# Stacked high and low halves for 512-column matmuls in the feed-forwards, and another order of the first expert tiles

## The chip, the cores and the metric

One core of a Trainium2 chip runs the whole program. The metric is the device time of one execution in microseconds (us), as a median of several runs; the profile is one further execution. TensorE (PE in the profile) multiplies, VectorE (DVE), ScalarE (ACT) and GpSimd (POOL) work elementwise, SyncE (SP) issues nearly all DMAs.

## The reference

A token sequence (256 tokens of width 1024) passes through five blocks. What is computed, cut to its core:

```python
x = x + hybrid_mixer(rms_norm(x))            # state-space part and attention, gated, three output projections
h = rms_norm(x)
gi = argmax(h @ w_rg); top2 of the 8 experts of that group
x = x + sum_over_experts(comb * (silu(h @ w_gate[e]) * (h @ w_up[e])) @ w_down[e])   # 32 experts, 2 a token
x = rms_norm(x + sigmoid(rms_norm(x) @ w_ple_gate) * (p @ w_ple))
for i, kind in enumerate((0, 1, 2, 0)):      # short conv, neighborhood attention, hyena, short conv
    x = x + mixer[kind](rmsnorm(x))
    x = x + (silu(g) * u) @ w2               # g, u = split(rmsnorm(x) @ w13); 1024 -> 2 x 2816 -> 1024
```

All of it is float32.

## The kernel before

Activations lie with features on the partitions and the 256 tokens along the free axis; a tile `(128, 2, 256)` holds a pair of feature blocks `o`. Weights are one stream `wst` in DRAM in the order of use. A tile of the stream is 128 x 1024 floats (512 KB): eight 128 x 128 blocks.

**Precision.** A float32 product is made of three matmuls in the fp32r format. A value is split into a high part (ScalarE, a copy that rounds) and a low part (VectorE, value minus high part): weights into `wh`, `wl`, activations into `hh`, `hl`. Each block then costs `wh*hh + wh*hl + wl*hh`, three matmuls of 256 columns with a weight load each (`dense`, line 690). `dense` goes over output pairs `j`; each has one PSUM bank out of four (`mm`), and for every input block `k` and `o` in 0, 1 it takes the next weight block (`block`, line 597). `evac` takes the bank away at the pair's end. While the norm of the input (`norm`, whose factor is applied to the output) isn't there, finished pairs are held.

**The feed-forward** (`ffn`, line 1856) is a dense of 22 pairs over 8 input blocks (`w13`: 22 x 16 = 352 weight blocks) and one of 4 pairs over 22 (`w2`: 176). After each `w13` pair VectorE multiplies the bank by the norm factor (`t`), ScalarE takes Silu of one half, VectorE multiplies the halves, and the result is split (`fh`, `fl`). After `w2`, `residual` (line 876) adds to `x` and prepares the next input and its sum of squares.

**Order.** The program is emitted by Python against a rough clock of its own. Side work (generators in `sides`) is emitted between matmuls by `pump`. Each engine then runs its own list in that order, and semaphores join them.

**Weight buffers.** `raw` has 7 buffers, `wh` and `wl` 5 each, `slots` 46 general ones of 128 x 512. `load_parts` (line 507) issues the next tile of the stream to SP.

**Experts.** In `moe` (line 1433) weights are used unsplit, as moving operand of plain float32 matmuls with 32 stationary columns, four side by side. The experts run in 8 rounds of 4; a round takes 8 tiles (`gate_up(r, 0)`), the 8 down tiles of the round before, and 8 more (`gate_up(r, 1)`). There are 192 tiles. While the router runs, tiles are loaded ahead: `early` (line 534) takes the first 13 free places of the stream in pairs of slots (`raws`), the raw buffers the next 7, and once the last dense is over the 5 + 5 split buffers hold raw tiles too. A tile used up from `raw`, `wh` or `wl` is loaded anew at once (`used_up`); one from slots is not.

Routing is a chain: last residual, `route_pair` (line 1413: transposes, then logits), norm factor, some 25 small VectorE steps to `sel`, counts (`cnt`), places (`ph`), gathers (`hg`), first `gate_up`. Work of the hyena filters (`filters`, line 2111) is stepped in by `next(filt)`, as 24 `fl` matmuls for two orders. `weights(0)` (matmul `cs`) stands in the middle of round 0. `past` (line 1577) reads the largest expert load and branches over a fallback on every engine; it stands at the start of round `r == 2`, after `moe_back` of the round before.

Of the kernel before, what the change touches and what calls it, by code (L numbers as in the profile page):

```python
# [271 lines left out]
NEARLY, EGAP = 13, 1.5  # L272
# [141 lines left out]
class Net:  # L414
    def __init__(self, ctx, tc, a, taps=None):
# [33 lines left out]
        self.nload = self.nsplit = self.ahead = 0  # L449
# [57 lines left out]
    def load_parts(self, parts, kind="raw"):  # L507
        if self.nload < len(self.order):
# [14 lines left out]
    def load_slots(self):  # L523

        c, half = self.order[self.nload]
        t = [self.new("raws", shape=(128, 512)) for _ in range(2)]
        self.raw[self.nload], self.kind[self.nload] = t, "slots"
        self.nload += 1
        self.ahead += 1
        for i in range(2):  # L530
            o = half * 1024 + i * 512
            self.nc.sync.dma_start(t[i], self.a["wst"][c][:, o:o + 512])

    def early(self, n):

        while self.nload < self.moe_tiles[0]:
            yield
        for _ in range(n):
            self.load_slots()
            t0 = self.now()  # L540
            while self.now() < t0 + EGAP:
                yield
# [147 lines left out]
    def dense(self, xh, xl, nk, npairs, evac, j0=0, norm=None, lead=1):  # L690
# [4 lines left out]
        for js in [range(j0, j0 + lead)] + [(j,) for j in range(j0 + lead, j0 + npairs)]:  # L695
            pss = [self.mm_tile("mm") for _ in js]
            for k0 in range(0, nk, 2):
                for ps in pss:
                    for k in (k0, k0 + 1):
                        a, b = xh(k), xl(k)  # L700
                        self.fill(a, b)
                        for o in range(2):
                            wh, wl = self.block()
                            for i, (w, x) in enumerate(((wh, a), (wh, b), (wl, a))):
                                nc.tensor.matmul(ps[:, o, :], w, x, start=(k == 0 and o == 0 and i == 0),
                                                 stop=(k == nk - 1 and i == 2), skip_group_check=True)
# [4 lines left out]
            held += zip(js, pss)  # L711
# [7 lines left out]
    def dense_halves(self, xh, xl, ready, evac):  # L719

        nc = self.nc
        pss = [None] * 4
        for hf in range(2):
            self.wait(lambda: ready(hf))
            for j in range(4):
                if hf == 0:
                    pss[j] = self.mm_tile("mm")
                for k in range(4 * hf, 4 * hf + 4):
                    a, b = xh(k), xl(k)
                    self.fill(a, b)  # L730
                    for o in range(2):
                        wh, wl = self.block()
                        for i, (w, x) in enumerate(((wh, a), (wh, b), (wl, a))):
                            nc.tensor.matmul(pss[j][:, o, :], w, x, start=(k == 0 and o == 0 and i == 0),
                                             stop=(k == 7 and i == 2), skip_group_check=True)
# [3 lines left out]
    def dense_rows(self, xh, xl, evac, chs):  # L739
        nc = self.nc  # L740
        for ch in chs:
            pss = [self.mm_tile("mmr", (128, 512)) for _ in range(2)]
            for k in range(8):
                wh, wl = self.block(512)
                for t in range(2):
                    a, b = xh(k)[:, t * 128:t * 128 + 128], xl(k)[:, t * 128:t * 128 + 128]
                    for i, (x, w) in enumerate(((a, wh), (a, wl), (b, wh))):
                        nc.tensor.matmul(pss[t], x, w, start=(k == 0 and i == 0), stop=(k == 7 and i == 2))
# [3 lines left out]
    def half(self, tiles):  # L752
        def f(k):
            if tiles[k // 2] is None:
                self.wait(lambda: tiles[k // 2] is not None)
            return tiles[k // 2][:, k % 2, :]
# [3 lines left out]
    def split_pair(self, src, scales, hi, lo):  # L760
        nc = self.nc
        for o in range(2):
            nc.scalar.activation(hi[:, o, :], src[:, o, :], AF.Copy, scale=scales[o])
        for o in range(2):
            nc.vector.scalar_tensor_tensor(lo[:, o, :], src[:, o, :], scales[o], hi[:, o, :].bitcast(F32),
                                           op0=ALU.mult, op1=ALU.subtract)
# [5 lines left out]
    def split_pair_steps(self, src, scales, hi, lo):  # L772
        nc = self.nc
        for o in range(2):
            nc.scalar.activation(hi[:, o, :], src[:, o, :], AF.Copy, scale=scales[o])
        yield
        for o in range(2):
            nc.vector.scalar_tensor_tensor(lo[:, o, :], src[:, o, :], scales[o], hi[:, o, :].bitcast(F32),
                                           op0=ALU.mult, op1=ALU.subtract)
# [29 lines left out]
    def prep_input(self, j, scales):  # L809
        if j == 0:  # L810
            self.hh, self.hl = [None] * 4, [None] * 4
        h, l = self.new("hh", F32R), self.new("hl", F32R)
        self.split_pair(self.x[j], scales, h, l)
        self.hh[j], self.hl[j] = h, l
# [8 lines left out]
    def gains(self, name, i, j):  # L823
        return [self.v(name, 8 * i + 2 * j + o) for o in range(2)]

# [56 lines left out]
    def setup(self):  # L882
# [11 lines left out]
        ps = self.sd("warm", (128, 128))  # L894
        for _ in range(WARM):
            nc.tensor.matmul(ps, self.ones, self.ones, start=True, stop=True)
# [81 lines left out]
    def hybrid(self):  # L978
        nc, v = self.nc, self.v
        V, S, G = nc.vector, nc.scalar, nc.gpsimd  # L980
        hh, hl = self.half(self.hh), self.half(self.hl)
# [37 lines left out]
        oh, ol = [None] * 4, [None] * 4  # L1019
# [17 lines left out]
        self.dense(hh, hl, 8, 1, lambda j, ps: tables.append(self.side(first(ps))))  # L1037
        self.side(self.ssd(hh, hl, X, BC, y))
        early = []
        self.dense_rows(hh, hl, lambda *a: early.append(a), (0,))  # L1040
# [6 lines left out]
        self.dense(hh, hl, 8, 2, evac, 1, norm=norm)  # L1047
# [1422 lines left out]
```

## Time and profile before

| | us |
| --- | --- |
| median of 3 runs (1856.04 to 1856.8) | 1856.15 |
| profiled execution | 1855.08 |
| its span, first to last instruction | 1853.3 |
| PE busy | 1784.5 (96%) |
| DVE busy | 1155.6 (62%) |
| ACT busy | 952.7 (51%) |
| POOL busy | 413.3 (22%) |

The page gives busy time by engine, 40 slices of the span with clock and DMA rate, and the chain of work that ended last. Busy spans of matmuls overlap, since they are pipelined: what a matmul costs in a stream is read from the distance of starts, not from its duration. PEclk is the granted TensorE clock, 1.00 for 2.4 GHz and 0.50 for 1.2 GHz.

### The profile page before, as it was taken

What the parts mean: (1) busy time and instruction counts of PE and PEld (TensorE: products, weight loads), DVE (VectorE), ACT (ScalarE), POOL (GpSimd) and SP (SyncE); (2) the same over time, 40 slices, a digit from 0 to 9 for tenths busy, and PEclk for the clock granted to TensorE, in tenths of its full rate; (3) what the DMA queues carried; (4) which work ended last, traced back from release to release, by engine and by line L of the source; (5) the groups of instructions that cost most, each with busy time, mean ns of one, the idle gap of its engine ahead of it and who ended that gap; (6) DMA issues with size and microseconds to landing.
All of it is one profiled execution on the core that took longest, in us unless ns stands there. A gap on an engine that the chain in (4) does not pass through costs nothing.

```text
span 1853.3 us, 34155 instructions
## 1 busy us (share of the span) xinstructions
PE 1784.5 (96%) x13779; PEld 1606.7 (87%) x13779; DVE 1155.6 (62%) x1603; ACT 952.7 (51%) x1515; POOL 413.3 (22%) x452
## 2 busy tenths in 40 slices
PE   9999999998888899999999999999899999999999
PEld 8897899542326899999987999998899999999999
DVE  6677665322125987665697666569976655676653
ACT  7887653331225655444566644466554444655442
POOL 4636340342441340000122000027610000500000
PEclk9999999899899999999999999999999999999999
DMA  8443359699998575555554455555345555555552
GB/s 295 148 132 120 128 182 337 251 362 406 409 406 296 166 243 183 183 183 185 180 165 135 131 184 183 176 193 196 129 129 189 183 183 181 183 180 185 182 185 77
DMA packets 115210, 377.39 MB, mean 204 GB/s; under 512 B 12480, under 2 KB 22088, under 8 KB 115048
## 3 DMA queue, kind: packets, MB, share of 16 engines
q1 hardware_dynamic: 114856, 375.03, 59.2%
q8 instruction: 109, 1.79, 0.4%
q14 instruction: 53, 0.43, 0.1%
q0 software_dynamic: 48, 0.13, 0.0%
q10 hardware_dynamic: 144, 0.00, 0.0%
HBM read 369.87 MB, written 5.25 MB: 202 GB/s over the span
## 4 chain that ended last, share of the span: by engine, by line
PE 66%; DMA 8%; DVE 2%; issue 2%; POOL 1%; ACT 1%; SPq 0%; POOLq 0%; DVEq 0%; ACTq 0%
PE mm L400 59%; DMA raw<-in_wst 8%; PE mmr L400 1%; PE ci L400 1%; PE s L400 1%; PE gu L400 1%; DVE wl L400 1%; PE U L400 1%; DMA dec<-in_decay 0%; PE po L400 0%; PE pt L400 0%; DVE l L400 0%; DVE rb L400 0%; PE hg L400 0%; PE yo L400 0%
## 5 line engine op out<-in xcount | busy, mean ns | idle before, releaser
L400 DVE TENSOR_TENSOR wl<-raw,wh 128x1024 fp32r<-128x1024 f32 (+1 forms) x486 | 611.8, 1266 | 325.7 <-ACT wh L400 325.4
L400 ACT ACTIVATE wh<-raw 128x1024 fp32r<-128x1024 f32 (+1 forms) x486 | 508.9, 1053 | 497.7 <-issue 285.7
L400 PE MATMUL mm<-hh,wh 128*128 128x256 f32 x2576 | 740.0, 287 | 7.6 <-ACT hh L400 5.4
L400 PE MATMUL mm<-hl,wh 128*128 128x256 f32 x2576 | 730.1, 283 | 0.8 <-DVE hl L400 0.7
L400 PE MATMUL mm<-hh,wl 128*128 128x256 f32 x2576 | 729.8, 283 | 0.4 <-DVE wl L400 0.4
L400 PEld LDWEIGHTS mm<-hh,wh 128*128 128x128 f32 x2576 | 495.0, 192 | 18.6 <-issue 8.5
L400 PEld LDWEIGHTS mm<-hl,wh 128*128 128x128 f32 x2576 | 495.2, 192 | 2.3 <-DVE hl L400 1.4
L400 PEld LDWEIGHTS mm<-hh,wl 128*128 128x128 f32 x2576 | 495.0, 192 | 0.9 <-DVE wl L400 0.9
L400 PE MATMUL mm<-fh,wh 128*128 128x256 f32 x704 | 199.2, 283 | 0.0
L400 PE MATMUL mm<-fl,wh 128*128 128x256 f32 x704 | 199.2, 283 | 0.0
L400 PE MATMUL mm<-fh,wl 128*128 128x256 f32 x704 | 199.2, 283 | 0.0
L400 POOL TENSOR_TENSOR acc<-acc,sq 128x512 f32<-128x512 f32 x20 | 31.8, 1590 | 705.6 <-DVE hl L400 318.3
L400 PEld LDWEIGHTS mm<-fh,wh 128*128 128x128 f32 x704 | 135.2, 192 | 0.0
L400 PEld LDWEIGHTS mm<-fl,wh 128*128 128x128 f32 x704 | 135.2, 192 | 0.0
L400 PEld LDWEIGHTS mm<-fh,wl 128*128 128x128 f32 x704 | 135.2, 192 | 0.0
L400 PE MATMUL gu<-raw,hg 128*32 128x512 f32 x464 | 93.6, 632 | 8.4 <-DMA raw<-in_wst 7.4
L400 DVE TENSOR_TENSOR t<-mm,rb 128x512 f32<-128x512 f32 x104 | 71.9, 691 | 29.4 <-PE mm L400 28.9
L400 PEld LDWEIGHTS gu<-raw,hg 128*32 128x32 f32 x464 | 18.8, 112 | 61.4 <-DMA raw<-in_wst 37.1
L400 ACT ACTIVATE hh<-x,vec 128x256 fp32r<-128x256 f32 x72 | 32.8, 503 | 65.5 <-DVE x L400 63.2
L400 PE MATMUL yo<-raw,hTs 128*32 128x512 f32 x252 | 53.0, 630 | 6.2 <-DMA raw<-in_wst 3.7
L400 PE MATMUL mm<-yh,wh 128*128 128x256 f32 x192 | 55.1, 287 | 0.0
L400 PE MATMUL mm<-yh,wl 128*128 128x256 f32 x192 | 54.3, 283 | 0.0
(404 smaller groups left out, 2660.8 us busy)
## 6 DMA issues: line engine op xcount, KB each, us to landing
raw<-in_wst SPq DMA_DIRECT2D x661, 512.0 KB, 4.8
raws<-in_wst SPq DMA_DIRECT2D x26, 256.0 KB, 7.0
hs<-H SPq DMA_DIRECT2D x16, 256.0 KB, 5.0
Hl<-hs SPq DMA_DIRECT2D x16, 256.0 KB, 8.5
tb<-in_rpbt SPq DMA_DIRECT2D x16, 192.0 KB, 2.6
dec<-in_decay SPq DMA_DIRECT2D x8, 256.0 KB, 5.4
x<-in_xT SPq DMA_DIRECT2D x4, 256.0 KB, 6.2
raw<-in_wst SPq DMA_DIRECT2D x4, 256.0 KB, 6.0
```

The source lines that it names most:

```text
L400: return f(*args, **kw)
```

## The change

**Stacked activations.** All activations that feed a dense are kept as one tile per block, `[:, 0, :]` high and `[:, 1, :]` low. With `wide=True` (all four feed-forwards, both denses; and the short conv of `i == 3`), a pair whose norm is there takes two banks, one for each `o`: a matmul of 512 columns `wh * (high, low)` and one of 256, `wl * high`, added onto the first half. At the pair's end ScalarE copies the second half and VectorE adds the first half, for each `o`, to a tile `mo`; `evac` goes on from there, in the feed-forward on GpSimd. Other denses keep three matmuls of 256 columns.

**Experts.** The slots take 11 tiles, the places 8 to 18 of the expert stream; the 7 before them go to `raw`. The branch stands after `gate_up(0, 1)`. Logits go before transposes; two idle fillers of dummy matmuls (`busy`) are put in; one order's `fl` matmuls go ahead of the router and the other's behind it; places 1 to 3 move to side work; the exponentials move up.

```diff
-NEARLY, EGAP = 13, 1.5
+NEARLY, EGAP = 11, 1.5
+        self.early_tiles = range(2 * m + NRAW, 2 * m + NRAW + NEARLY)
     def load_parts(self, parts, kind="raw"):
+        if self.nload in self.early_tiles:
+            self.nload = self.early_tiles[-1] + 1
...
-            if c and self.nload - self.ahead < c + NRAW:
+            if c and self.nload < c + NRAW:
...
     def dense(self, x, nk, npairs, evac, j0=0, norm=None, lead=1, wide=False):
+            two = wide and len(js) == 1 and norm not in self.sides
+            pss = [[self.mm_tile("mm") for _ in range(2 if two else 1)] for _ in js]
...
+                            if two:
+                                nc.tensor.matmul(ps[o].rearrange("p a b -> p (a b)"), wh, xk.rearrange("p a b -> p (a b)"),
+                                                 start=(k == 0), stop=False, skip_group_check=True)
+                                nc.tensor.matmul(ps[o][:, 0, :], wl, xk[:, 0, :], start=False, stop=(k == nk - 1),
+                                                 skip_group_check=True)
+                            else:
+                                self.three(ps[0][:, o, :], wh, wl, xk, k == 0 and o == 0, k == nk - 1)
...
+            if two:
+                t = self.new("mo")
+                for o in range(2):
+                    nc.scalar.activation(t[:, o, :], pss[0][o][:, 1, :], AF.Copy)
+                    nc.vector.tensor_tensor(t[:, o, :], t[:, o, :], pss[0][o][:, 0, :], op=ALU.add)
+                held.append((js[0], t))
...
+    def busy(self, n):
+        ps = self.sd("warm", (128, 128))
+        for _ in range(n):
+            self.nc.tensor.matmul(ps, self.ones, self.ones, start=True, stop=True)
...
     def ffn(self, i, next_scales):
         def evac(j, ps):
             t = self.new("t")
-            V.tensor_tensor(t, ps, self.rbb(), op=ALU.mult)
+            (V if ps.space == PSUM else nc.gpsimd).tensor_tensor(t, ps, self.rbb(), op=ALU.mult)
...
     def moe(self):
+        next(filt)
+        next(filt)
         self.load()
...
         V.reciprocal(rt, rt)
-        next(filt)
-        next(filt)
+        self.busy(12)
...
-        next(filt)
-        next(filt)
+        self.busy(4)
         tp = m("tp", 2, 32)
...
-        next(filt)
-        next(filt)
-        for q in range(1, 4):
-            places(q)
...
         for r in range(8):
-            if r == 2:
-                self.finish(back.pop())
-                past()
...
             if r == 0:
+                past()
                 self.side(later())
```

## Rows read from the trace of the kernel before

**Rows 1.** The page's first line.

```profile
span 1853.3 us, 34155 instructions
```

**Rows 2.** Chain of waits, pieces in order: start us, us, what.

```profile
462.70 9.63 DMA raw<-in_wst
...
714.03 189.35 PE mm L400 x1578
...
1045.04 188.63 PE mm L400 x1572
...
1381.61 188.63 PE mm L400 x1572
```

**Rows 3.** Timeline of PE, 256 then 512 columns: start us, us, engine, what.

```profile
1258.81 0.28 PE L400 MATMUL mm<-hh,wl 128*128 128x256 f32 x1
1258.93 0.40 PE L400 MATMUL U<-h,dfth 128*128 128x512 f32 x1
...
1260.32 0.28 PE L400 MATMUL mm<-hh,wh 128*128 128x256 f32 x1
```

**Rows 4.** Timeline of PE, a run of 512-column matmuls.

```profile
976.08 0.40 PE L400 MATMUL mmr<-wh,hh 128*128 128x512 f32 x1
...
979.27 0.39 PE L400 MATMUL mmr<-wh,hl 128*128 128x512 f32 x1
```

**Rows 5.** Groups in the last w13, 1664:1785: busy us, mean ns, idle before.

```profile
L400 DVE TENSOR_TENSOR wl<-raw,wh 128x1024 fp32r<-128x1024 f32 x43 | 52.7, 1225 | 32.7 <-ACT wh L400 32.7
L400 DVE TENSOR_TENSOR t<-mm,rb 128x512 f32<-128x512 f32 x21 | 14.5, 692 | 6.4 <-PE mm L400 6.3
L400 DVE TENSOR_TENSOR fl<-t,fh 128x256 fp32r<-128x256 f32 x21 | 8.8, 419 | 0.0
L400 ACT ACTIVATE fh<-t 128x256 fp32r<-128x256 f32 x21 | 8.4, 401 | 0.0
```

**Rows 6.** Busy by window: us, PE, PEld, DVE, ACT, POOL (count), clock, DMA share, GB/s.

```profile
1664.00:1760.00 96.00, 96.00 (x802) 96.00 (x802) 65.17 (x85) 47.25 (x69) 0.00 (x0) 1.00 0.58 187
```

**Rows 7.** Groups in the hyena stage, 1258:1350, where POOL works beside DVE.

```profile
L400 DVE TENSOR_TENSOR wl<-raw,wh 128x1024 fp32r<-128x1024 f32 x17 | 27.3, 1610 | 0.0
L400 POOL TENSOR_TENSOR cm<-cm 128x512 f32<-128x512 f32 x16 | 25.4, 1606 | 17.8 <-DVE cm L400 17.8
```

**Rows 8.** Timeline of DVE where a dense ends and the last w13 begins.

```profile
1658.54 0.69 DVE L400 TENSOR_TENSOR x<-x,mm 128x512 f32<-128x512 f32 x1
1659.81 0.89 DVE L400 SCALAR_TENSOR_TENSOR hl<-x,vec,hh 128x256 fp32r<-128x256 f32 x2 [0.58 <-ACT hh L400]
...
1664.52 1.75 DVE L400 RECIPROCAL rb<-rb 128x256 f32<-128x256 f32 x1 [0.30 <-ACT rb L400]
```

**Rows 9.** Busy by window around routing and the first expert rounds, columns as above.

```profile
320.00:330.00 10.00, 7.59 (x41) 7.33 (x42) 3.79 (x16) 0.60 (x1) 0.00 (x0) 0.55 0.60 237
330.00:340.00 10.00, 5.68 (x47) 2.81 (x46) 8.59 (x21) 3.78 (x6) 4.83 (x6) 0.96 0.46 140
340.00:350.00 10.00, 10.00 (x64) 3.26 (x68) 1.04 (x5) 1.07 (x2) 2.54 (x2) 0.70 0.47 153
...
380.00:390.00 10.00, 10.00 (x85) 6.88 (x83) 1.35 (x6) 5.38 (x11) 1.53 (x3) 1.00 0.62 224
...
430.00:440.00 10.00, 8.86 (x46) 1.81 (x39) 0.54 (x2) 0.47 (x1) 0.00 (x0) 1.00 1.02 409
```

**Rows 10.** Timeline of DVE: the places of the first gather.

```profile
323.03 0.69 DVE L400 TENSOR_TENSOR ph<-cst,r_tp 128x512 fp32r<-128x512 f32 x1
```

**Rows 11.** Timeline of PE: first gather, first gate and up, weights of round 0.

```profile
325.51 0.79 PE L400 MATMUL hg<-ph,hth 128*128 128x256 f32 x2
...
331.51 0.62 PE L400 MATMUL gu<-raws,hg 128*32 128x512 f32 x2 [0.43 <-DVE F L400]
...
339.05 1.75 PE L400 MATMUL cs<-r_cw,ph 128*128 128x5 f32 x8 [3.89 <-DVE r_most L400]
```

**Rows 12.** Timeline of SP around the branch, 371:392.

```profile
375.76 0.30 SPq L400 DMA_DIRECT2D hn<-hn  x1
384.86 5.62 SPq L400 DMA_DIRECT2D raw<-in_wst  x10
```

More of the change, by code (lines that the diff above doesn't have):

```diff
@@ L521, in load_parts, with early @@
                 yield
[L523 to L534, printed above, removed]
+    def early(self):
         while self.nload < self.moe_tiles[0]:
             yield
-        for _ in range(n):
-            self.load_slots()
+        for n in self.early_tiles:
+            c, half = self.order[n]
+            t = [self.new("raws", shape=(128, 512)) for _ in range(2)]
+            self.raw[n], self.kind[n] = t, "slots"
+            for i in range(2):
+                o = half * 1024 + i * 512
+                self.nc.sync.dma_start(t[i], self.a["wst"][c][:, o:o + 512])
             t0 = self.now()
@@ L687, in drain, with dense @@
         self.wait(lambda: not self.sides)
-    def dense(self, xh, xl, nk, npairs, evac, j0=0, norm=None, lead=1):
+    def dense(self, x, nk, npairs, evac, j0=0, norm=None, lead=1, wide=False):
         nc = self.nc
@@ L717, in dense, with three, dense_halves @@
                 held = []
-    def dense_halves(self, xh, xl, ready, evac):
-        nc = self.nc
+    def three(self, ps, wh, wl, xk, start, stop):
+        for i, (w, h) in enumerate(((wh, 0), (wh, 1), (wl, 0))):
+            self.nc.tensor.matmul(ps, w, xk[:, h, :], start=(start and i == 0), stop=(stop and i == 2), skip_group_check=True)
+    def dense_halves(self, x, ready, evac):
         pss = [None] * 4
@@ L893, in setup @@
         nc.scalar.activation(warm, self.eps, AF.Copy)
-        ps = self.sd("warm", (128, 128))
-        for _ in range(WARM):
-            nc.tensor.matmul(ps, self.ones, self.ones, start=True, stop=True)
+        self.busy(WARM)
         first = itertools.chain(self.load_parts(2), self.load_parts(2))
@@ L1690, in ple_evac @@
             S.activation(self.pp[j], ps, AF.Copy)
-        self.dense(lambda k: pth[:, k, :], lambda k: ptl[:, k, :], 2, 4, ple_evac)
-        self.wait(lambda: self.hh[0] is not None)
+        self.dense(self.each(px), 2, 4, ple_evac)
+        self.wait(lambda: self.hx[0] is not None)
     def moe_back(self, r, yo, pT):
@@ L1818, in gate @@
                 self.fsum = self.fold(self.accf)
-        self.dense(self.half(old[0]), self.half(old[1]), 8, 4, evac, norm=norm, lead=3)
-        self.wait(lambda: self.hh[0] is not None and self.hh[0] is not old[0][0])
+        self.dense(self.each(old), 8, 4, evac, norm=norm, lead=3)
+        self.wait(lambda: self.hx is not old and self.hx[0] is not None)
     def final_norm(self):
@@ L1873, in act @@
             yield
-            yield from self.split_steps(t[:, 0, :], hid_h[j // 2][:, j % 2, :], hid_l[j // 2][:, j % 2, :])
+            f = self.new("fx", F32R)
+            yield from self.split_steps(t[:, 0, :], f[:, 0, :], f[:, 1, :])
+            hid[j] = f
             done.append(j)
-        self.dense(self.half(self.hh), self.half(self.hl), 8, 22, evac, norm=self.rms())
+        self.dense(self.each(self.hx), 8, 22, evac, norm=self.rms(), wide=True)
         self.wait(lambda: len(done) == 22)
-        self.dense(self.half(hid_h), self.half(hid_l), 22, 4,
-                   lambda j, ps: self.residual(ps, j, next_scales(j) if next_scales else None))
+        self.dense(self.each(hid), 22, 4,
+                   lambda j, ps: self.residual(ps, j, next_scales(j) if next_scales else None), wide=True)
         for j in range(4):
@@ L1939, in split @@
         def split(j):
-            h, l = self.new("yh", F32R), self.new("yl", F32R)
-            yield from self.split_steps(cv[j], h, l)
-            yh[j], yl[j] = h, l
-        self.dense(self.half(self.hh), self.half(self.hl), 8, 12, scaled, norm=norm, lead=1 if i else 3)
-        self.dense(self.half(yh), self.half(yl), 8, 4, lambda j, ps: self.residual(ps, j, self.gains("ffn", i, j)))
+            yx[2 * j:2 * j + 2] = yield from self.split_both(cv[j], "yx")
+        self.dense(self.each(self.hx), 8, 12, scaled, norm=norm, lead=1 if i else 3, wide=i > 0)
+        self.dense(self.each(yx), 8, 4, lambda j, ps: self.residual(ps, j, self.gains("ffn", i, j)), wide=i > 0)
         for j in range(4):
```

256 lines of the change are left out of this document (118 added, 138 removed).

## The prediction

> **What bounds the kernel now.** I read the chain of waits first. It has two kinds of stretch. From the first short conv on it is an unbroken run of `mm` matmuls, three pieces of some 1570 being the feed-forwards [rows 2]: 188.63 us / 1572 = 120.0 ns a matmul, so TensorE's own stream sets the time there and nothing waits. In the expert stage the chain is DMA of weight tiles [rows 2], at 409 GB/s and a full DMA share [rows 9]; a tile of 524 KB then takes 1.28 us. The windows show where this stream is not full: 237, 140 and 153 GB/s between 320 and 350 us, and 224 between 380 and 390 [rows 9]. Against 409 these lose 4.2 + 6.6 + 6.3 + 4.5 = 21.6 us. As the stream is full from there to the end of the experts, each us of it not lost brings the end of the experts forward by as much. So the change has to be priced twice: by matmul spacing, and by idle DMA.
>
> **Wide matmuls.** Per weight block the old form takes 3 x 120 = 360 ns. The new one is one matmul of 512 columns and one of 256. The trace has both spacings: 256 columns 1258.93 - 1258.81 = 120 ns, 512 columns (1260.32 - 1258.93) / 6 = 232 ns in a group of six between other work [rows 3], and (979.27 - 976.08) / 14 = 228 ns in a long run [rows 4]. So two matmuls of 256 (240 ns) become 228 to 232, and a block is cheaper by 8 to 12 ns. I take 11, near to the long run, since the feed-forwards are long runs too.
>
> How many blocks: a pair goes wide only if the norm is there when it starts. The norm's reciprocal starts 6.0 us after the residual that closes the dense before and takes 1.75 [rows 8], a pair takes 16 x 0.36 = 5.8 us, so pairs 0 and 1 stay narrow. A feed-forward has 20 x 16 + 176 = 496 wide blocks, four have 1984; the last short conv has 10 x 16 + 64 = 224. Together 2208 x 11 ns = 24.3 us; bounds 2208 x 8 = 17.7 and 2208 x 12 = 26.5. One more narrow pair in each of the five stages would take back 5 x 16 x 11 ns = 0.9 us.
>
> The Trainium skill has a formula for this, "TensorE: Matmul & The Clock Gate", section "Back-to-back issue gap": a warm isolated matmul takes N/2.4 + 2.5 ns, that is 109 and 216 ns, so only the 2.5 ns would be saved per block, an estimate of 5.5 us in all. The rows differ: 120 and 228 to 232 ns.
>
> What it adds: per wide pair two ScalarE copies and two VectorE adds of 256 columns, 0.40 and 0.42 us each by the rows nearest in size, while VectorE loses the `t` product of 0.69 to GpSimd [rows 5]. In `w13` VectorE is busy 65.17 of 96 us and ScalarE 47.25 [rows 6]: 3.9 and 2.8 us per pair of 5.76. They become about 4.1 and 3.6 in a pair of 5.6. Both fit, and the weights are split several tiles ahead, so I cost this at nothing inside a dense. The GpSimd product is new beside VectorE; its price is the third rival.
>
> At the end of a wide dense the way to `x` grows by copy, add, add and their links, 0.4 + 0.42 + 0.42 + 0.1 = 1.3 us. Between stages it is hidden: the low part of the next input is complete 1660.70 - 1658.54 = 2.2 us after the last sum starts [rows 8], and the next dense works on its first six input blocks for 12 x 0.36 = 4.3 us before it needs it. At the very end nothing hides it: + 1.3 us. If the cover were short by 0.5 us at each of four joints, another 2.
>
> **The experts.** First the start of the first round. Places (`ph`) are ready at 323.03 + 0.69 = 323.7, but the gather starts at 325.51 behind 12 `fl` matmuls at half the clock (0.55 in this window), and `gu` follows at 331.51 [rows 9 to 11]. Those `fl` go. Against it, logits now stand before the transposes, and the last transposed tile still has to be copied and split before the norm factor can be emitted, on ScalarE and VectorE, about 1 us more ahead of the chain. So the gather starts at about 324.8. Its 32 matmuls take 3.8 us at full clock, 5.6 as now. The dummy matmuls fill the idle time ahead; whether they hold 2.4 GHz no row can say. `gu` at 328.7 to 330.4; I take 329.
>
> Then the refill. At present the tiles from slots lie among the first places and give no refill, so little is loaded up to 345 us. Now places 1 to 7 are refilled as the first half round uses them: seven loads, 9 us of DMA from about 331.5 to 340.5. Places 8 to 18 give none, until the next round. The matmul `cs`, which waited 3.89 us for VectorE [rows 11], is ready in time, as the filter's products and three `places` leave its way. Round 0 ends at about 337.5 and tiles that can be refilled come free at 340 to 342.
>
> The branch: SP issues nothing from 376.06 to 384.86, 8.8 us [rows 12], and that is the hole of 380 to 390 us. Now it follows the seven loads on SP's list, at about 333.5, and SP is back at 342.3. DMA has work until 340.5, so it stands for some 2.5 us in place of 4.5. The other engines have their own copy of the branch; TensorE takes it between rounds, where it would wait for SP's tiles in any case.
>
> Idle DMA after: 325 to 331.5 and 340.5 to 343, 9 us, with 0.6 for ramps 9.6, against 21.6: a gain of 12 us. Bounds: a gather at half clock and 5 us more at the branch, gain 5; the branch wholly covered, 15. The number of tiles that lie ready is 28 in the new order, and two of the old 30 were issued only after the first round had begun, so nothing is lost there. The rest of the new expert order (places and exponentials moved) is off the path once the DMA stream binds.
>
> **Sum.** On the profiled execution, 1855.08 us (its span 1853.3 [rows 1] plus what lies around it): - 24.3 - 12 + 1.3 = - 35, giving 1820.1. The median lies 1.07 above that execution: 1821 us. Bounds of this case: - 26.5 - 15 + 1.3 gives 1816, - 17.7 - 5 + 3.3 gives 1837.
>
> **Rivals.** *The expert gain is lost.* If SP's branch must wait for something that the old place gave for free, or the gather stays on a cold clock and DMA then stands through the branch, the idle DMA only moves. For it: the 8.8 us of SP [rows 12] are as long as the work queued ahead of them. Against it: that queue is counted from tiles, not guessed. A gain of 3 instead of 12: 1830 us.
>
> *The 512-column form saves only a fixed trifle of 2 to 3 ns a block.* Then 2208 x 2.5 ns = 5.5 us is left: 1856 - 12 - 5.5 + 1.3 = 1840 us. Both runs of 512 columns speak against it [rows 3, 4]; for it, neither has the two sizes alternating. It is what the formula named above would give.
>
> *VectorE becomes the bound in `w13`, and the kernel is slower.* Where GpSimd works beside it, the same VectorE split takes 1610 ns instead of 1225 [rows 5, 7]: the two get in each other's way when both inputs are in SBUF. The Trainium skill says so too ("SBUF — State Buffer", section "Who interferes with whom"): a VectorE instruction with two SBUF inputs contends with a GpSimd one that reads SBUF, and one blocks wholly. The trace agrees in kind (1610 against 1225). Per wide pair VectorE would need 4.1 us of work, up to 1.6 locked out [rows 7], 0.3 waiting for the last matmul [rows 5] and 0.4 for the ScalarE copy: 6.4 us, where the pair's matmuls need 5.6. That is 0.8 x 80 pairs = 64 us more, about 1885. It binds from 5.6 on and turns the sum's sign at 6.0. Against it: each wait counted here can hide another, as in the present `w13`, where VectorE already idles 2 us a pair [rows 5], and mean excess in hyena is 0.39 an operation, not 1.6: 4.1 + 2 x 0.39 + 0.7 = 5.6, just at the edge. A small part of this loss may come without the sign turning; that is why the range reaches further up than down.
>
> **Chances.** Forecast 0.74, expert gain lost 0.12, trifle 0.07, VectorE bound 0.07 (of it slower by over 0.2% 0.05, within 0.2% 0.02). The range is 1813 to 1841: it takes in the bounds of the forecast and the first two rivals and leaves the third out. A difference under 0.2% (3.7 us) can't be told from none here. Faster 0.93, same 0.02, slower 0.05.
>
> **What would show it.** The chain's feed-forward pieces should shrink from 188.6 to about 183 us each, with 512-column `mm` starts 228 to 232 ns apart and no VectorE idle time ended by GpSimd on the path. `gu` should start near 329; the windows 330 to 340 should be near 400 GB/s, and the hole of 380 to 390 gone, with a small one near 341. The prediction is wrong if waits for `wl` or `mo` appear on TensorE in `w13`, if the 512-column spacing is near 240, or if a hole of 10 us follows the branch.

## The result and the profile after

The changed kernel takes **1832.47 us** (median of 4 runs, 1830.64 to 1834.63) against 1856.10 for the kernel before beside it: a ratio of **0.9875** (95% interval 0.986 to 0.989), 23.6 us less. The forecast was 1821 us, with a range of 1813 to 1841. The sign and the range held. The sum promised 35 us and two thirds of it came, so most of what follows asks where the rest went. The profiled execution took 1834.63 us.

The page of after, first line and busy shares (us, share of the span, instructions):

```profile
span 1832.8 us, 30301 instructions
PE 1764.5 (96%) x11603; PEld 1491.7 (81%) x11603; DVE 1252.2 (68%) x1758; ACT 1019.1 (56%) x1754; POOL 514.1 (28%) x532
```

3854 instructions fewer than before [rows 1]. TensorE is still busy nearly all the time, so its spacing still prices the later stages.

**Wide matmuls.** Timeline of PE in the second `w13`, after (start us, us, engine, what):

```profile
1099.76 0.40 PE L400 MATMUL mm<-hx,wh 128*128 128x512 f32 x1
1100.00 0.28 PE L400 MATMUL mm<-hx,wl 128*128 128x256 f32 x1
1100.11 0.40 PE L400 MATMUL mm<-hx,wh 128*128 128x512 f32 x1
1100.35 0.28 PE L400 MATMUL mm<-hx,wl 128*128 128x256 f32 x1
...
1101.53 0.40 PE L400 MATMUL mm<-hx,wh 128*128 128x512 f32 x1
```

Read the starts, not the durations, which overlap. From 1099.76 to 1101.53 lie five weight blocks: 354 ns each. Over all 1440 blocks of `hx` the 512-column matmul is followed after 236.4 ns and the 256-column one after 116.9: 353.3 ns in place of 360, so 6.7 ns saved where the sum had 11. And the joints between stages (here the third feed-forward, from its first matmul through the change of dense to the next stage):

```profile
1361.69 0.40 PE L400 MATMUL mm<-hx,wh 128*128 128x256 f32 x2
...
1486.58 0.28 PE L400 MATMUL mm<-hx,wl 128*128 128x256 f32 x1
1486.70 0.40 PE L400 MATMUL mm<-fx,wh 128*128 128x512 f32 x1
...
1548.76 0.28 PE L400 MATMUL mm<-fx,wl 128*128 128x256 f32 x1
1548.88 0.40 PE L400 MATMUL mm<-hx,wh 128*128 128x256 f32 x2
```

The same stage before, first matmul and change to the next stage:

```profile
1375.26 0.28 PE L400 MATMUL mm<-hh,wh 128*128 128x256 f32 x1
...
1565.76 0.28 PE L400 MATMUL mm<-hh,wh 128*128 128x256 f32 x1
```

The stage takes 1548.88 - 1361.69 = 187.19 us; before it took 1565.76 - 1375.26 = 190.50. The 3.31 us saved are 496 blocks of 6.7 ns, and the next dense follows the last matmul after 0.12 us, as inside a dense: the longer way to `x` is hidden there, as argued.

**Experts.** Busy by window, after (columns as in [rows 9]):

```profile
320.00:325.00 5.00, 5.00 (x30) 4.83 (x30) 3.00 (x19) 2.23 (x4) 0.00 (x0) 0.66 1.03 409
325.00:330.00 5.00, 3.27 (x29) 3.06 (x29) 4.30 (x24) 2.30 (x5) 0.00 (x0) 1.00 0.37 143
330.00:335.00 5.00, 5.00 (x46) 2.84 (x48) 1.05 (x2) 1.79 (x3) 1.04 (x2) 1.00 0.03 7
335.00:340.00 5.00, 5.00 (x48) 1.91 (x40) 0.56 (x4) 0.00 (x0) 0.44 (x1) 1.00 0.85 259
340.00:345.00 5.00, 0.54 (x8) 0.23 (x8) 1.51 (x2) 0.47 (x1) 4.84 (x6) 0.89 1.03 398
345.00:350.00 5.00, 5.00 (x36) 1.28 (x28) 0.00 (x0) 0.60 (x1) 0.35 (x1) 0.77 0.36 124
350.00:360.00 10.00, 10.00 (x82) 5.03 (x79) 0.00 (x0) 3.21 (x6) 1.28 (x1) 1.00 0.97 343
...
380.00:390.00 10.00, 8.89 (x62) 6.95 (x65) 1.40 (x4) 3.98 (x8) 7.42 (x9) 0.83 1.03 409
```

The last two columns are the DMA share and GB/s. The hole at 380 to 390 is gone. A new one stands at 345 to 360. Against 409 GB/s the windows lose 3.3 + 4.9 + 1.8 + 0.1 + 3.5 + 1.6 = 15.2 us, where those of before lost 21.6 [rows 9]: 6.4 won by this count, where 12 were forecast. (The count takes in that routing itself began 2.9 us later in this execution, see the ledger.) Where the engines were at that time, PE and then SP:

```profile
328.00 0.51 PE L400 MATMUL hg<-ph,hth 128*128 128x256 f32 x2
332.03 2.35 PE L400 MATMUL gu<-raw,hg 128*32 128x512 f32 x19
335.60 1.05 PE L400 MATMUL cs<-r_cw,ph 128*128 128x5 f32 x8
336.59 3.64 PE L400 MATMUL gu<-raws,hg 128*32 128x512 f32 x32
344.69 1.07 PE L400 MATMUL gu<-raws,hg 128*32 128x512 f32 x2 [4.46 <-PEq L1594]
```

```profile
333.97 18.14 SPq L400 DMA_DIRECT2D raw<-in_wst  x13
337.72 11.16 SPq L400 DMA_DIRECT2D raw<-in_wst  x3
```

`cs` waits for nothing now [rows 11]. But line 1594, the branch, holds TensorE's sequencer (`PEq`): the compare-and-branch is recorded at 338.12 with 6.25 us, where before it was 0.45. On SP the second row covers three loads, the first at 337.72 and the next only at 348.06: loading the condition starts at 338.25 and the branch comes at 339.10. What SP does behind it: its instructions of line 1594 (count, ns, first and last start), then its waits from 337 to 349 us (us in total, times, longest). The third row is the same branch in the kernel before:

```profile
L1594 SPq EVENT_SEMAPHORE  x8: 17/17/17, 344.1 to 347.9; - x8
```

```profile
SPq L1594 <- SPq L1594: 8.5, 4, 5.0
```

```profile
L1581 SPq EVENT_SEMAPHORE  x8: 17/17/17, 379.5 to 384.7; - x8
```

Each of the eight waits for a semaphore on which SP's loads tell that they have landed, and adds to it (so the view names the line itself as what it waits for). Four of them have to wait. They end at 344.14, 345.19, 346.44 and 347.68 us; the last loads on these four semaphores were issued at 335.34, 335.99, 336.74 and 337.72, 8.8 to 10.0 us earlier, and the trace has the last of them landing at 347.64. So SP stands at the branch until all that it has in flight has landed, and when it goes on DMA is empty: nothing moves from 347.5 to 349 us. Before, five of the eight waited, each until 9.5 to 10.2 us after the issue of its load.

The first SP row above says when refill begins: 333.97, 1.94 us after `gu`.

**A ledger by stages** of the two profiled executions, from the starts of the first and last matmuls or sums of each stage:

| stage | before us | after us | difference |
|---|---|---|---|
| start to last sum before routing | 313.86 | 316.77 | +2.9 |
| from there to the last `yo` | 254.69 | 245.94 | -8.75 |
| last `yo` to first `w13` | 139.85 | 140.19 | +0.3 |
| four feed-forwards up to their last matmul | 761.9 | 749.0 | -12.8 |
| neighborhood | 139.78 | 138.37 | -1.4 |
| hyena | 146.08 | 146.04 | 0.0 |
| last short conv | 92.58 | 91.09 | -1.5 |
| last matmul to the end | 4.60 | 5.39 | +0.8 |

They add up to the 20.5 us between the two spans. The first line was in no forecast; the experiments say what it is.

### The profile page after: what moved, and what is told of

It is laid out like the page before. It is cut to its first block, busy times and chain, and to the rows that moved or that the text cites. A ratio compares the mean times of both kernels' runs of the same rounds, so it can differ in the third digit from the quotient of the medians.

```text
span 1832.8 us, 30301 instructions
## 1 busy us (share of the span) xinstructions
PE 1764.5 (96%) x11603; PEld 1491.7 (81%) x11603; DVE 1252.2 (68%) x1758; ACT 1019.1 (56%) x1754; POOL 514.1 (28%) x532
## 5 line engine op out<-in xcount | busy, mean ns | idle before, releaser
L400 PE MATMUL mm<-hx,wh 128*128 128x256 f32 (+1 forms) x3712 | 936.1, 331 | 7.3 <-ACT hx L400 5.1
L400 PE MATMUL mm<-hx,wl 128*128 128x256 f32 x2576 | 727.6, 282 | 0.6 <-DVE wl L400 0.6
L400 PEld LDWEIGHTS mm<-hx,wh 128*128 128x128 f32 x3712 | 628.4, 191 | 86.8 <-issue 8.5
L400 PEld LDWEIGHTS mm<-hx,wl 128*128 128x128 f32 x2576 | 491.0, 191 | 1.2 <-DVE wl L400 1.2
L400 PE MATMUL mm<-fx,wh 128*128 128x512 f32 x704 | 248.9, 399 | 0.0
L400 POOL TENSOR_TENSOR t<-mo,rb 128x512 f32<-128x512 f32 x80 | 103.5, 1293 | 406.1 <-DVE mo L400 393.0
L400 PE MATMUL mm<-fx,wl 128*128 128x256 f32 x704 | 197.7, 281 | 0.0
L400 PEld LDWEIGHTS mm<-fx,wh 128*128 128x128 f32 x704 | 132.3, 188 | 33.0
L400 PEld LDWEIGHTS mm<-fx,wl 128*128 128x128 f32 x704 | 133.0, 189 | 0.0
L400 DVE TENSOR_TENSOR mo<-mo,mm 128x256 f32<-128x256 f32 x220 | 82.5, 416 | 21.3 <-ACT mo L400 21.3
## 6 DMA issues: line engine op xcount, KB each, us to landing
Hl<-hs SPq DMA_DIRECT2D x16, 256.0 KB, 11.3
```

What stands on the lines that cost most here:

```text
L400: return f(*args, **kw)
```

## The experiments

Each ratio is against the kernel before, run on the same chip beside it; after has 0.9875.

**How much is the wide form worth?**

```
-            two = wide and len(js) == 1 and norm not in self.sides
+            two = False
```

> The changed kernel with the wide form switched off everywhere (three matmuls of 256 columns for each weight block, product of the feed-forward on VectorE as before); the new expert order and place of the branch stay. Theory A, from the spacing in the trace of after: a wide block takes 236.4 + 117 = 353.3 ns in place of 360, 6.7 ns for 2208 blocks = 14.8 us, so 1832.5 + 14.8 = 1847. Theory B, the term of the prediction (11 ns, 24 us): 1856, which would leave nothing for the experts. Theory C, a fixed trifle of 2.5 ns (5.5 us): 1838.

1842.45 us, ratio 0.9919 (0.9902 to 0.9936): 0.0044 or 8 us above after. B is out; by the total alone C (0.990) fits and A (0.995) does not. The trace says otherwise: the first three feed-forwards, narrow now, take 190.50 us again, each 3.31 more, as A has it, but the last sum before routing comes 1.9 us earlier than in after's trace, and hyena, which has no wide matmul in either, takes 143.4 in place of 146.0. A's price holds to 0.01 us in these three stages; the total mixes it with stages that moved for other reasons.

**What costs 236 ns?**

```
-for each output o:  wh[o] 512 columns, wl[o] 256 columns
+for each output o:  wh[o] 512 columns
+for each output o:  wl[o] 256 columns
```

> The changed kernel with the wide form's matmuls grouped by size: for each input block first the two of 512 columns, then the two of 256 (512, 512, 256, 256 in place of 512, 256, 512, 256). Theory A, a change of size is what costs: the spacing in a run of 512 columns is 227 to 228 ns and in a run of 256 it is 120, so two blocks take at best 228 + 236 + 120 + 117 = 701 in place of 706.8, 1104 x 6 = 6 us less, 1826; with no cost of changing at all 695, 13 us less, 1819.5. Theory B, the 236 ns are the price of a 512-column matmul whose next weights come after a short one, and grouping changes nothing: 1832.5 within 0.1%.

1822.56 us, ratio **0.982** (0.9804 to 0.9836): about 10 us faster than after, and by the ratio 33 faster than before. Timeline of PE in the second `w13` of the grouped version, where each row covers two matmuls:

```profile
1099.64 0.62 PE L400 MATMUL mm<-hx,wh 128*128 128x512 f32 x2
1100.10 0.40 PE L400 MATMUL mm<-hx,wl 128*128 128x256 f32 x2
1100.33 0.63 PE L400 MATMUL mm<-hx,wh 128*128 128x512 f32 x2
...
1101.73 0.63 PE L400 MATMUL mm<-hx,wh 128*128 128x512 f32 x2
```

Six blocks from 1099.64 to 1101.73: 348 ns each. The means are 232.9, 233.3, 114.6 and 115.8 ns, 696.7 for two blocks against 706.7. A feed-forward takes 184.7 us in place of 187.2. That is 11.7 ns a block saved against the old form, what the prediction had; theory A holds.

**Size or bank?** The grouped order also changes the PSUM bank with every matmul. Here four matmuls in a row write one bank:

```
-per input block:  wh[0], wh[1] (512), wl[0], wl[1] (256)
+per two input blocks and output o:  wh, wh (512), wl, wl (256), all into the bank of o
```

> The grouped version again (two matmuls of 512 columns, then two of 256), but each four accumulate into one PSUM bank: two input blocks of the first output, then two of the second. In the grouped run the banks alternated with every matmul, so its gain may come from the size or from the bank. Theory A, sizes in a row are what helps: the four spacings stay 233, 233, 115, 116 ns (697 ns for two blocks) and the time is that of the grouped run, 0.982 of before, 1822.5. Theory B, a matmul that follows one into another bank starts sooner: within a bank the spacings go back to 236 and 117 to 120 (706 ns), 1830 to 1832.

The spacings are the same to 0.1 ns (232.9, 233.3, 114.6, 115.8) and each of the first three `w13` takes 123.29 us in both. So it is the sizes in a row, not the bank: theory A. Yet the time is 1834.61 us, ratio 0.9883 (0.9867 to 0.99), 12 us more than the grouped version. Between the two profiled executions it is 14.0 us, and 11.3 of them are hyena: 157.9 us in place of 146.6. Its waits of PE there (us in total, times, longest):

```profile
PE ci L400 <- DVE cm L400: 8.6, 1, 8.6
```

In the grouped version the same wait is 0.4. The two programs give VectorE and GpSimd their side work in a different order, since that order is set by a modelled clock which the new matmul order shifts. No matmul of hyena was touched. Why the new order is worse was not settled.

**The branch, taken out and put back.**

```
             if r == 0:
-                past()
```

> The changed kernel without the branch: the part for experts with more than 32 tokens, which this input never enters, and the loading of its condition are left out. Theory A, SP's silence from 338 to 348 us causes the idle DMA of 345 to 360 us (5.1 us by windows of 5 us): 1832.5 - 5 = 1827.5, and gu of round 1 goes on near 338.5 in place of 344.7. Theory B, the idle DMA comes from the places that give no refill, and SP has nothing to issue then anyway: 1832, with the hole still there.

1826.04 us, ratio 0.9836 (0.9819 to 0.9852). Its windows:

```profile
330.00:335.00 5.00, 5.00 (x48) 2.21 (x50) 0.00 (x0) 0.70 (x2) 1.99 (x4) 1.00 0.33 75
335.00:340.00 5.00, 5.00 (x48) 1.36 (x48) 1.35 (x6) 0.47 (x1) 3.71 (x4) 1.00 0.91 308
340.00:345.00 5.00, 5.00 (x46) 2.44 (x46) 0.82 (x1) 1.58 (x3) 0.28 (x1) 1.00 1.02 415
345.00:350.00 5.00, 5.00 (x48) 2.48 (x39) 0.00 (x0) 1.12 (x2) 1.28 (x1) 1.00 1.02 410
```

The hole of 345 to 360 is gone and DMA stays full from 340 on; first `gu` to last `yo` takes 224.85 us in place of 230.68. So the branch costs 5.8 us at the new place: theory A. Left is the idle DMA up to 340 us, 9.9 us by the windows from 325 on, which no branch makes.

```
+            if r == 2:
+                self.finish(back.pop())
+                past()
...
             if r == 0:
-                past()
```

> The changed kernel with the branch back at its old place, ahead of round 2 and behind the end of the work of round 0. Theory A, the new place is the better one because SP's silent time falls where DMA has had its loads already: the hole of 380 to 390 us comes back (4.5 us), the idle time at 340 to 350 gets less by at most 3, so 1834 to 1837. Theory B, the new place is the worse one, because TensorE now stands 6.25 us in the branch and SP until 348 us while nothing has been loaded ahead: the old place saves some 3 us, 1829. Theory C, both places cost the same: within 0.1% of 1832.5.

1830.46 us, ratio 0.986 (0.9844 to 0.9876), an interval that overlaps after's; the median lies between theory B and the lower edge of C, so the time alone doesn't choose. Its windows where the branch now lies:

```profile
360.00:370.00 10.00, 7.95 (x57) 5.21 (x55) 2.75 (x4) 1.79 (x3) 0.00 (x0) 1.00 1.03 408
370.00:380.00 10.00, 10.00 (x60) 6.35 (x64) 1.84 (x6) 1.90 (x4) 6.17 (x8) 0.66 0.54 173
```

A hole of 10 x (1 - 173/409) = 5.8 us, the same price in another place. SP's branch is at 365.57 and its next load at 374.67, 9.1 us, against 9.0 at the new place (339.10 to 348.06). The semaphores are again what it waits for, here two of the eight, until 11.1 us after the issue of each load; the others had landed:

```profile
L1594 SPq EVENT_SEMAPHORE  x8: 17/17/17, 372.9 to 374.5; - x8
```

So in all three traces the branch empties the stream of loads, wherever it stands. TensorE's own branch takes 0.35 us here, not 6.25, and it makes no difference: first `gu` to last `yo` takes 229.87 us in place of 230.68. Theory C, by the ledger; the rest of the 2 us lies ahead of routing, where the two programs don't differ and their traces do: 313.21 against 316.77 for the last sum.

That is also the ledger's first line. Over the traces of after and of its variants that sum falls between 313.0 and 316.8. In after's trace the granted clock is 0.57 between 16 and 20 us, in the late-branch trace it is 1.00 there:

```profile
16.00:20.00 4.00, 3.25 (x8) 2.63 (x9) 3.97 (x5) 2.58 (x4) 3.11 (x4) 0.57 1.04 395
```

```profile
16.00:20.00 4.00, 3.83 (x17) 3.17 (x18) 3.97 (x6) 1.98 (x3) 3.71 (x4) 1.00 1.05 396
```

The first `ssq` follows at 23.5 and 21.5 us. The clock falls a second time at 64 us in after's trace, and not in the late-branch one:

```profile
64.00:68.00 4.00, 4.00 (x26) 3.81 (x24) 2.87 (x6) 3.23 (x5) 3.59 (x7) 0.57 0.03 10
```

```profile
64.00:68.00 4.00, 4.00 (x38) 3.81 (x37) 1.60 (x2) 3.96 (x10) 3.66 (x5) 1.00 0.36 108
```

Over the traces of this case the last sum goes with these two stretches: 313.0 to 314.1 us without either (before's 313.86 among them), 314.6 to 315.4 with one of them (near 17 or near 62 us), 316.3 to 316.8 with both. So the 2.9 us came from one execution to the next and not from the change.

**The places of the early tiles.**

```
-NEARLY, EGAP = 11, 1.5
+NEARLY, EGAP = 13, 1.5
...
-        self.early_tiles = range(2 * m + NRAW, 2 * m + NRAW + NEARLY)
+        tiles 2 * m to 2 * m + NEARLY - 1, taken and counted as before
```

> The changed kernel with the early expert tiles at places 1 to 13 as before (NEARLY 13, taken in order) in place of 8 to 18; everything else as in the change. Theory A, the refill is what the experts gained: between the first gu and 350 us little is loaded again, as before, some 6.3 us of idle DMA come back, but part of it now lies beside the 5 us in which SP stands in the branch, so + 3 to + 6: 1835.5 to 1838.5. Theory B, the gain came from the earlier gather and the branch's place, and the places don't matter: 1832.5 within 0.1%.

1836.69 us, ratio 0.99 (0.988 to 0.9921). The last sum to the last `yo` takes 249.81 us, 3.9 more than after: theory A, and the time is inside its range. But only 2.0 of the 3.9 lie behind `gu`, where the refill acts (first `gu` to last `yo` 232.68 us against 230.68). The other 1.9 lie ahead of it: the gather took 5.9 us in place of 4.0, at a granted clock of 0.63 in place of 1.00, with the dummy matmuls in. Whether the old places bring this clock or only this execution had it is not shown.

**The dummy matmuls.**

```
-        self.busy(12)
...
-        self.busy(4)
```

> The changed kernel without the 12 and 4 dummy matmuls in the routing. Theory A, they hold the clock: without them the granted clock in 325 to 340 us falls from 1.00 to about 0.55 as in the kernel before, the gather's 32 matmuls take 5.6 us in place of 3.8 and gu starts 2 us later, which the weight stream passes on: 1834.5. Theory B, the clock comes from the filter's and the gather's own work, and gu starts at the same distance from the last residual, 15.3 us: 1832.5 within 0.1%.

1834.32 us, ratio 0.9887 (0.9867 to 0.9907), which can't be told from after. The trace can: the gather starts 10.83 us after the last sum (after: 11.24), but its 32 matmuls take 6.4 us in place of 4.0, and `gu` starts at 17.20 in place of 15.26. Its windows, with the granted clock third from the right:

```profile
320.00:325.00 5.00, 0.32 (x4) 0.21 (x4) 4.39 (x28) 1.79 (x4) 0.00 (x0) 0.59 0.97 381
325.00:330.00 5.00, 4.32 (x20) 4.35 (x21) 3.44 (x15) 2.12 (x4) 1.02 (x2) 0.50 0.09 33
```

After has 0.66 and 1.00 there. In this run TensorE, left idle, comes to the gather at 1.2 GHz; in after's, kept busy, it comes at 2.4. That is not so in every execution: with the same dummies the gather took 4.0 to 4.9 us in the traces of the other variants (granted clock over it 0.79 to 1.00), and 5.9 with the old places. The last `yo` comes 1.5 us later after the last sum than in after, so the dummies are worth about that: theory A in kind. The size is rough, since variants that leave this stretch alone spread over 1.8 us in it (244.9 to 246.7).

**VectorE and GpSimd.**

```
-            (V if ps.space == PSUM else nc.gpsimd).tensor_tensor(t, ps, self.rbb(), op=ALU.mult)
+            V.tensor_tensor(t, ps, self.rbb(), op=ALU.mult)
```

> The changed kernel with the feed-forward's product by the norm factor on VectorE in place of GpSimd. Theory A, VectorE has room in w13 and GpSimd's contention is paid out of it: wl goes from a mean of 1411 ns back towards 1266, and the time stays 1832.5 within 0.1%. Theory B, VectorE is at its edge: 0.4 to 0.7 us more per pair with 0.9 idle, less what contention gives back; if any of it shows it is up to 0.2 x 80 = 16 us, 1848. Theory C, the contention costs time at the joints now: up to 2 us faster, 1830.5.

1831.93 us, ratio 0.9879 (0.9858 to 0.99): the same, and all four `w13` are as long as in after (124.89 us, the last 125.3). Groups of VectorE and GpSimd in the last `w13`, first after (1646 to 1765 us), then with the product on VectorE (the same 691 matmuls, 1641.12 to 1760.12 us):

```profile
L400 DVE TENSOR_TENSOR wl<-raw,wh 128x1024 fp32r<-128x1024 f32 x45 | 70.7, 1578 | 9.7 <-ACT wh L400 9.0
L400 POOL TENSOR_TENSOR t<-mo,rb 128x512 f32<-128x512 f32 x19 | 24.5, 1290 | 97.8 <-DVE mo L400 97.8
```

```profile
L400 DVE TENSOR_TENSOR wl<-raw,wh 128x1024 fp32r<-128x1024 f32 x45 | 54.7, 1222 | 16.1 <-ACT wh L400 16.1
L400 DVE TENSOR_TENSOR t<-mo,rb 128x512 f32<-128x512 f32 x19 | 13.1, 692 | 0.7
```

GpSimd takes 19 products off VectorE, 13.1 us, and makes the 45 splits 0.356 us longer each, 16 us. VectorE is busier with the help than without: 100.59 of 119 us against 96.96. The move to GpSimd frees nothing here.

```
                 for o in range(2):
                     nc.scalar.activation(t[:, o, :], pss[0][o][:, 1, :], AF.Copy)
+                    if nk == 8:
+                        nc.vector.tensor_tensor(t[:, o, :], t[:, o, :], t[:, o, :], op=ALU.max)
                     nc.vector.tensor_tensor(t[:, o, :], t[:, o, :], pss[0][o][:, 0, :], op=ALU.add)
```

> The changed kernel with two more VectorE instructions of 256 columns, both inputs in SBUF, per wide pair of the input denses (a maximum of the copied half with itself, which changes no value), ahead of the two adds. By the nearest row, some 0.42 us each, 0.84 a pair; VectorE idles about 0.89 a pair of 5.68 in after. Theory A, it still just fits, and only the 80 joints between pairs can show it: 1832.5 to 1834. Theory B, the contention with GpSimd grows with it and VectorE becomes the bound: each 0.1 us that does not fit costs 80 x 0.1 = 8 us, so 1840 or more, with waits for wl on TensorE in w13.

1843.40 us, ratio 0.9939 (0.9919 to 0.9959), 11 us more, and none of it in the first three `w13`: they take 124.89 us as in after. It is all in the last short conv (98.2 in place of 91.1 us) and the `w13` behind it (129.3 in place of 125.4). PE's two largest waits from 1547 to 1775 us in this run; in after's trace the same stretch has none:

```profile
PE mm L400 <- DVE yx L400: 3.8, 1, 3.8
PE mm L400 <- DVE wl L400: 2.2, 2, 1.3
```

So three of the four `w13` have room for the added VectorE work (0.42 us an instruction here too, 0.83 a pair), and the last short conv has not. Theory A for three stages, B for the short conv; whether the `w13` behind it is short by itself or still pays for the short conv is not shown. Where the contention falls moves too: in the last `w13` `wl` is back at 1266 ns while the 256-column `fx<-t,fx` went from 425 to 1395:

```profile
L400 DVE TENSOR_TENSOR fx<-t,fx 128x256 fp32r<-128x256 f32 x18 | 25.1, 1395 | 0.0
L400 POOL TENSOR_TENSOR t<-mo,rb 128x512 f32<-128x512 f32 x17 | 36.4, 2142 | 79.6 <-DVE mo L400 76.0 <-ACT wh L400 3.6
```

**More wide stages.** On the grouped version:

```
-        self.dense(self.each(self.hx), 8, 12, scaled, ..., wide=i > 0)
+        self.dense(self.each(self.hx), 8, 12, scaled, ..., wide=True)
...
+        wide=True in the input denses of neighborhood and hyena
```

> The grouped version with the wide form in three more stages: the first short conv, and the input denses of the neighborhood mixer and of hyena (about 9, 6 and 10 pairs of 16 blocks, and 64 blocks of the first short conv's second dense). Theory A, TensorE sets these stages too: 12 ns a block, so up to 2.4, 1.1 and 1.9 us less, 1817. Theory B, VectorE is as near to its edge there as the last short conv has shown (0.84 us more per pair cost 7 us in it): each of the stages gets longer, by up to 0.84 us for each of 25 pairs = 21 us less the gain, 1825 to 1838.

1852.83 us, ratio 0.9985 (0.9971 to 0.9999): nearly all of the grouped version's gain is lost again. Stage by stage against the grouped version: last `yo` to the first `w13` 147.9 in place of 138.3 us, neighborhood 149.3 in place of 137.9, hyena 162.7 in place of 146.6. Theory B, and past its bound. These stages are of the profiled execution, the slowest of ten (1859.55 us). How much of hyena's 16 us the wide form itself costs is not shown: in the same-bank run another order of side work alone cost 11.3 us there. In hyena VectorE is fully busy, TensorE is busy for 6.74 of 10 us, and the granted clock is at half:

```profile
1323.00:1333.00 10.00, 6.74 (x28) 6.18 (x29) 10.00 (x14) 5.54 (x13) 5.91 (x4) 0.52 0.22 67
```

**The first two pairs.**

```
-            two = wide and len(js) == 1 and norm not in self.sides
+            two = wide and len(js) == 1
```

> The grouped version with pairs 0 and 1 of each wide dense in the wide form too, though the norm's factor is not there yet (the added halves wait in SBUF in place of PSUM). Theory A, only matmul spacing counts: 5 stages x 32 blocks x 12 ns = 1.9 us less, 1820.5. Theory B, VectorE and ScalarE have no time at a joint, where they split the next input: the first pairs wait, and the time stays or grows by some 0.5 us a joint, 1822.5 to 1825.

1822.94 us, ratio 0.9815 (0.9799 to 0.9832), not to be told from the grouped version. The first three `w13` take 122.95, 122.92 and 122.92 us in place of 123.29, which is 32 blocks of 11.5 ns, and nothing waits at the joints; in its profiled execution the stages ahead of the first `w13` took 5 us longer, so the total can't confirm the 1.9 us. Theory A by the stage; the time by itself lies in theory B's range, and gives no verdict.

**Grouped, with the branch at the old place.**

> The grouped version with the branch at its old place, ahead of round 2. Theory A, the two edits add: matmuls by size gave 12 us, and the place of the branch is neutral between gu and the last yo (230 us either way; without the branch it was 225), so 1820 to 1823, ratio to before 0.981 to 0.982. Theory B, the old place is better by the 2 us that its run seemed to show: 1819 to 1820.5, ratio 0.980.

1823.38 us, ratio 0.9828 (0.9815 to 0.9842): theory A, if 0.4 us above its range. The place of the branch is neutral a second time. The fastest versions are the grouped ones, 1823 us.

## Why the prediction was right, and where it was off

**The bound** was read rightly: matmul spacing from the first short conv on, weight transfers in the experts. The price of the wide form could be read from the starts of matmuls to 0.1 us in the first three feed-forwards.

**Count of blocks**: right. There are 1440 wide blocks of `hx`, 704 of `fx` and 64 of `yx`, 2208; the first two pairs of each input dense are narrow.

**Price of a block**: this is the term that was mis-sized, 11 ns for 6.7. Here 24.3 us of the sum became 14.8 (2208 x 6.7 ns), below the lower bound of 17.7. The rows [rows 3, 4] are true, and the spacings in the changed kernel were worked out from runs of one size, while the change alternates. The prediction named just this under the second rival ("neither has the two sizes alternating") and didn't carry it into the bounds. The grouped version shows the term would have been right for two and two: 11.7 ns. Of the prediction's own signs of being wrong, a 512-column spacing near 240, this one came close: 236.4. What in TensorE makes a change of size dear is not known from these runs; the bank does not.

The formula quoted in the prediction from the Trainium skill ("TensorE: Matmul & The Clock Gate", "Back-to-back issue gap"), which is for an isolated matmul, came out at 2.5 ns a block; 6.7 and 11.7 were measured, both above it.

**Inside a dense and at the joints at nothing**: right. No wait of PE over 40 ns inside a wide dense of after, and 0.12 us from one dense to the next; only the last `w13` is 0.4 us longer than the others, around its `ssq`. **At the very end** 0.8 us where 1.3 were forecast.

**Start of the experts**: right in distance. `gu` was forecast at 329, 15.1 us after the last sum; it came at 15.26 us (before 17.65). It stood at 332.03 because that sum itself came 2.9 us later in this execution. In this execution the dummies held 2.4 GHz (granted clock 1.00 over the gather), which no row could say, and without them 1.9 us of the 2.4 are gone; in the trace of the old places they did not hold it (0.63).

**Refill**: right in kind, late in time. The seven loads were forecast from 331.5; SP issued the first at 333.97, since `gu` starts with 16 matmuls on four tiles that come free together, and the bytes follow later still: 7 GB/s in 330 to 335 and 259 in 335 to 340, where "near 400" was forecast. The old places cost 3.9 us, and 2.0 of these lie behind `gu`: that is what the runs show for the refill, of the 8.75 won.

**The branch**: wrong, in the mechanism. The prediction took SP's 8.8 us [rows 12] (7.8 from the branch itself) as a fixed time that the branch takes, so that loads issued just before it would cover it: SP back at 342.3, with 2.5 us uncovered. What SP waits for is the landing of those very loads, some 10 us from the issue of the last one, so that DMA has always run empty when SP comes back. SP reached the branch late, since the seven loads were issued from 333.97 to 337.72, each after its tile was used; it was back at 348.06, 0.4 us after the last had landed, and 5.8 us were uncovered. The first rival had named this ("as long as the work queued ahead of them"), and [rows 2] have a load that takes 9.63 us. Before, the branch was priced at 4.5, and put back it costs 5.8. So the move gained nothing. Of the 8.75 us, 2.4 lie ahead of `gu` and 6.4 behind it. The runs give 2.0 of the latter to the places and about 1.5 of the former to the dummies; the other 5 or so are left, by subtraction, for the reordering of the routing and were not tried alone. TensorE's 6.25 us in the branch were taken as harmless because it would wait for SP's tiles in any case; the late branch, without that wait, is not faster, so this step held.

**The rivals.** The expert gain was not lost: 8.75 of 12, inside its bounds, though the first rival's mechanism at the branch was the true one. The trifle of 2.5 ns was not it, though the truth lay half-way to it. VectorE did not become the bound in `w13`. But its parts are real: GpSimd beside it made `wl` 1578 ns in place of 1222. The Trainium skill's rule ("SBUF — State Buffer", "Who interferes with whom") agrees with that. The prediction counted 5.6 us a pair "just at the edge"; the run with 0.83 us more shows the edge lies beyond that in three of the four `w13` and within it in the last short conv. With the wide form in the first short conv, neighborhood and hyena too, nearly all of the gain was lost.

**Sum.** By the ledger the wide form gave 14.3, 10.0 less than forecast, the experts 3.3 less; the start of the profiled execution took 2.9 and the stretch ahead of the first `w13` 0.3. The other way, the neighborhood mixer, which was not in the sum, gave 1.4 and the end 0.5. That is 14.6 us, the way from 1820.1 to the 1834.63 of the profiled execution; the median lies 2.2 below it. The range held although the price of a block lay outside its own bounds: the bounds of the other terms and the first rival's 1830 left room for the shortfall, and that much is luck.

## What to carry to other kernels

Take a matmul's price from a run with the same sequence of sizes, and where sizes must mix, put equal ones side by side: here the order alone was worth 10 us. Price an edit stage by stage, since a program whose side work is ordered by a modelled clock can move an untouched stage by 11 us, as much as the edit itself. Before moving a branch that the loading engine takes, look at what that engine waits for behind it: here every load in flight, so the place didn't matter and only leaving it out gained (5.8 us). Handing VectorE work with SBUF inputs to GpSimd is no relief until the slower neighbours are counted.

## What was not expected of the hardware

- TensorE, same work, three orders: 360 ns a block as three of 256 columns, 353.3 as 512 and 256 in turn, 348.3 as two and two. In the last the second of two 256-column matmuls follows after 114.6 ns, less than the 120 of a long run.
- At the branch SP waits for every load that it has in flight to land. From its branch to its next load it took 9.0 us after, 9.1 with the late branch and 7.8 before, and each wait ended 8.8 to 11.1 us after the issue of the load that it waited for.
- The compare-and-branch on TensorE took 6.25 us at one place and 0.35 to 0.45 at another. Within the 6.25 us of after the trace has packets on two instruction queues (16 KB at 341.97 us, 8 KB at 343.14), so code loading may be the reason; no run took it away by itself.
- The slowing of VectorE beside GpSimd goes to whichever of its instructions meets it: with other work in between, a 256-column subtraction took 1395 ns in place of 425, and the product on GpSimd 2142 in place of 1290.
